# Hyena convolutions on one core: second-stage products of 512 columns, block turns spread over four chunks, and a capped stream of filter pieces

## The chip, the cores and the metric

The kernel runs on one core of one Trainium2 chip. The metric is the device time of one execution in microseconds; the time of a kernel is the median of its runs. The engines are named as in the profile: PE (TensorE, matmuls and transposes through the array), DVE (VectorE), ACT (ScalarE), POOL (GpSimd) and SP (SyncE, which here only issues DMAs).

## What is computed

One layer of a hybrid encoder on a sequence of 2048 positions: a Hyena branch and an RWKV branch side by side, joined by gates, then a feed-forward block. The change touches only the Hyena branch, after the projection of its input `u` to 3 x 512 channels:

```python
def long_conv(z, h_fwd, h_bwd, d_skip):
    L = z.shape[1]
    n = 2 * L
    zf = jnp.fft.rfft(z, n=n, axis=1)
    hf = jnp.fft.rfft(h_fwd, n=n, axis=0) + jnp.conj(jnp.fft.rfft(h_bwd, n=n, axis=0))
    y = jnp.fft.irfft(zf * hf[None], n=n, axis=1)[:, :L]
    return y + z * d_skip

def hyena_mixer(u, conv_w, conv_b, ..., skip):
    u = short_conv3(u, conv_w, conv_b)
    v, x1, x2 = jnp.split(u, 3, axis=-1)
    h = hyena_filters(L, ...)
    z = x1 * long_conv(v, h[:, 0, 0], h[:, 0, 1], sk[0])
    return x2 * long_conv(z, h[:, 1, 0], h[:, 1, 1], sk[1])
```

Each of the two long convolutions is made for four blocks of 128 channels: eight products of spectra in all. `hyena_filters` makes the filters from positions: sines, a matrix product and a decaying window.

## The kernel before

The stage is the function `hyena`, some 500 of 3946 us. A Fourier transform of 4096 points is made as matmuls in two stages of 128 x 32. The loop runs over eight products k = 0 to 7 and in each over eight chunks q = 0 to 7 of 128 x 512 numbers; (k,q) is chunk q of product k. In a chunk PE does, in this order:

- T (`times`): second stage of the transform of the signal, `second(V)`, into a PSUM tile `pz`. DVE multiplies it by the filter's spectrum H (the tile A, L1339) and by H with blocks of 32 partitions exchanged (the tile B, L1340). The exchange (Hs) is four DMAs from SP, L1329.
- L (`load`): the same for the spectrum of the filter, two chunks ahead, `second(Vf)`; ACT copies it to H.
- Q (`added`): the product back through the inverse of the second stage, for the chunk before, into `pq`; ACT copies it to Q.
- then the work that `beside` has put into the chunk, a list of functions per chunk.

`second` makes four matmuls of 128 columns (one weight, `Mc[:, 3]`, but `Mc[:, 0]` for the very first 128 columns of the spectrum), `added` eight. The matmuls are f32, and the trace has two records of each. The work beside:

- F: one of the 16 pieces of a filter: g0 g1 f0 g2 f1 ... g7 f6 f7. A g is a PE product (L1240, `pg`) that DVE multiplies by the window (L1244); an f is its first transform stage (L1226, `pf`), which needs the result of that g; ACT copies it (L1228) and sends it to DRAM as Hd (L1229, a DMA from ACT's queue). `given` (L1319) reads Hd back as Vf once all 16 pieces are made.
- turns: `turned`, four per product: four transposes on PE into `ph` (tag po, two PSUM buffers) and an ACT copy (L1286). They turn a row of 128 channels for the next product.
- U: `onward`, the first transform stage of the next product (L1294, matmuls on 64 rows, `pfz`); ACT copies.
- V: block transpositions of 32 x 32 on DVE (L1303, 2.1 to 2.3 us each). Four belong to the way back (`piece`, chunks 0 and 1) and four to the next product (`flipped`); T of (k+1,0) needs all four of the latter.
- i, v and gate: the last inverse stage (L1358), and in the products of the second convolution (k = 3, 4, 7) the turn back on PE (L1365, `pv`, buffers shared with `pq`) and the multiplication by x2 on DVE (L1370).
- conv: a block of 512 positions of the short convolution: ACT (L1183), then DVE (L1184, L1189).

The PSUM tag pf has two buffers, shared by pg, pf and pfz. On PE, ACT, DVE and SP the order of this stage is the order of the program text (`manual_schedule`): an instruction that waits holds all behind it on its engine. In product 6, `ready` adds the splitting of the weights of the next stage (`weights_on`: ACT and DVE, wl<-wr), in product 7 `late_inputs` the rest of it.

Of the kernel before, what the change touches and what calls it, by code (L numbers as in the profile page):

```python
# [190 lines left out]
class Layer:  # L191
# [943 lines left out]
    def next(self, name):  # L1135
        first, n = dict(w=(8, 3), A=(12, 2), B=(0, 2), H=(2, 3), Hs=(5, 3))[name]
        k = self.turns[name]
        self.turns[name] = k + 1
        return self.ring(first + k % n).rearrange("p (a b) -> p a b", b=P)
# [125 lines left out]
    def hyena(self):  # L1265
# [3 lines left out]
        N = 2 * HT  # L1269
        E = mybir.EngineType  # L1270
        with tc.tile_pool(name="hy", bufs=1, reuse_waits="tile") as s, tc.tile_pool(name="hyp", bufs=2, space=PSUM, reuse_waits="tile") as ps, \
# [26 lines left out]
            def flips(U, k):  # L1298
# [4 lines left out]
                    nc.vector.transpose(V[:, :, sl].rearrange("p j c -> p c j"), U[:, :, sl].rearrange("p n c -> p c n"))  # L1303
                return V, piece

            def second(v, q):
                p = ps.tile([P, 4, P], F32, name="pz", tag="pz")
                for j in range(4):
                    mm(p[:, j], Mc[:, 0 if 4 * q + j == 0 else 3], v[:, j], start=True, stop=True)  # L1309
                return p  # L1310


# [30 lines left out]
            def added(i, q, Q):  # L1343
                A, B = AB.pop((i, q))
                p = ps.tile([P, 4, P], F32, name="pq", tag="pq")
                for j in range(4):
                    m = 0 if 4 * q + j == 0 else 3
                    mm(p[:, j], Mc[:, m + 1], A[:, j], start=True, stop=False)
                    mm(p[:, j], Mc[:, m + 2], B[:, j], start=False, stop=True)
                nc.scalar.copy(Q[:, 4 * q:4 * q + 4], p)  # L1350


# [38 lines left out]

            most = 15, 20, 24, 29, 36, 41, 46, 48

            def F():
                self.upto(self.pieces + 1)


            def beside(k, Q):
                at = {q: [] for q in range(8)}

                def put(q, *fs):
                    at[q] += fs

                def conv():
                    if self.blocks < most[k]:
                        next(self.conv)

                on = k + 1 < N
                c, o = PRODUCTS[k - 1] if k else (1 - 2, 1)
                new = {}  # L1410

                def turned(q, src):
                    if q == 0:
                        new["z"] = zt(src)
                        new["o"] = self.z1 if k == 0 else self.short(HT + c if o == 0 else c + 2)
                    turn(new["o"], new["z"], q)

                def onward(q):
                    if q == 0:
                        new["U"] = self.pre(k + 1)  # L1420
                    fwd(new["z"], new["U"], q)

                def flipped(q):
                    if q == 0:
                        Vs[k + 1], new["f"] = flips(new["U"], k + 1)
                    new["f"](q)

                if k:
                    VQ, piece = flips(Q, k + 1)
                    f = [lambda q=q: piece(q) for q in range(4)]  # L1430
                    put(0, f[0], F, F, f[1], F)
                    put(1, f[2], F, F, f[3], F)
                else:
                    put(0, F, F, conv, F)
                    put(1, F, F, conv, F)
                t = [lambda q=q: turned(q, "x1" if k and o == 0 else "z") for q in range(4)]
                u = [lambda q=q: onward(q) for q in range(4)]
                if k and o == 0:
                    def inner(q):
                        if q == 0:  # L1440
                            new["x"], new["z"] = new["z"], zt("z")
                        p = inverse(VQ, q)
                        tt(out=new["z"][:, 4 * q:4 * q + 4], in0=p, in1=new["x"][:, 4 * q:4 * q + 4], op=ALU.mult)

                    n = [lambda q=q: inner(q) for q in range(4)]
                    put(1, t[0], t[1])
                    put(2, t[2], t[3], conv, n[0], n[1])
                    put(3, n[2], u[0], n[3], conv, u[1])
                    put(4, u[2], conv, u[3], F)
                else:  # L1450
                    if on:
                        put(1, t[0], t[1])
                        put(2, t[2], t[3])
                    if k:
                        result, turn_back, gated, ws = outward(k - 1, VQ)
                        r, b, g = ([lambda q=q, h=h: h(q) for q in range(4)] for h in (result, turn_back, gated))
                        if k > 3:
                            put(1, conv)
                        put(2, r[0], conv, r[1], F)
                        if on:  # L1460
                            put(3, r[2], u[0], r[3], b[0], conv, g[0], u[1])
                            put(4, b[1], u[2], g[1], b[2], u[3], conv, g[2], F)
                            put(5, b[3])
                        else:
                            put(3, r[2], b[0], r[3], g[0], b[1])
                            put(4, g[1], b[2], g[2], b[3], g[3])
                    else:
                        put(2, conv)
                        put(3, u[0], u[1], conv)
                        put(4, u[2], conv, u[3], F)  # L1470
                if on:
                    f = [lambda q=q: flipped(q) for q in range(4)]
                    put(5, f[0], F, F, conv, F)
                    if k and o:
                        put(5, g[3])
                    put(6, f[1], F, F, f[2], F)
                    if k == 4:
                        put(6, conv)
                    put(7, f[3], F, conv, F)
                return at  # L1480

# [10 lines left out]
            for q in range(4):  # L1492
                piece(q)
                if q < 2:
                    load(0, q)
                F()
                F()
            for k in range(N):
                Qs[k] = self.pre(k)
                at = beside(k, Qs.get(k - 1))  # L1500
                if k == N - 2:
                    self.ready(at)
                if k == N - 1:
                    self.late_inputs(at, ps)
                for q in range(8):
                    times(k, q, Vs[k])
                    n, r = divmod(q + 2, 8)
                    if k + n < N:
                        load(k + n, r)
                    if k or q:  # L1510
                        added(*((k, q - 1, Qs[k]) if q else (k - 1, 7, Qs[k - 1])))
                    for f in at[q]:
                        f()
                    if q in (3, 6) and k + 1 < N:
                        given(k + 1, q // 4)
            added(N - 1, 7, Qs[N - 1])
            self.outputs()
            VQ, piece = flips(Qs[N - 1], N)
# [16 lines left out]
    def ready(self, at):  # L1535
        nc = self.nc

        def first():
            self.wr = [self.xp1.tile([P, 8, 4, P], F32R, name=f"w{n}", tag=f"x{n}", bufs=1) for n in "hl"]
            self.wraws = [self.weights_raw("r", dt) for dt in range(2)]  # L1540

        at[4].append(first)
        for dt, q in enumerate((5, 6, 6, 7, 7)):
            at[q].append(lambda dt=dt: self.weights_on(dt))

    def weights_on(self, dt):
# [5 lines left out]
    def late_inputs(self, at, ps):  # L1552
        nc = self.nc

        def loads():
            row = self.pre(0)
            self.gates = row[:, 0:14]
            self.yraw = row[:, 16:24].rearrange("p a b -> p (a b)").rearrange("p (k t) -> p k t", t=TB)
            nc.sync.dma_start(self.yraw, self.yrd[:, :, 0:TB].rearrange("c p t -> p c t"))
            for dt in range(7):  # L1560
                nc.sync.dma_start(self.gates[:, 2 * dt:2 * dt + 2].rearrange("p a b -> p (a b)"), self.gated[8 + dt, :, 0:TB])

        def parts():
            hl = [self.wp.tile([P, 4, TB], F32R, name="y", tag="wh", bufs=2) for k in range(2)]
            self.split(*hl, self.yraw)
            self.yr = [(hl[0][:, k], hl[1][:, k]) for k in range(4)]

        def gates():
            nc.scalar.activation(self.gates, self.gates, AF.Tanh, scale=0.5)
            self.rs = [self.wp.tile([P, 4, TB], F32, name="rs", tag="wraw", bufs=2)]  # L1570

        for q in range(3):
            at[q].append(lambda q=q: self.weights_on(5 + q))
        at[2].append(loads)
        at[4].append(parts)
        at[4].append(gates)
        for q in range(3):
            at[5 + q].append(lambda q=q: self.right(ps, q))
# [298 lines left out]
```

## Time and profile before

| | us |
|---|---|
| three runs | 3939.88, 3943.91, 3944.74 (median 3943.91) |
| profiled execution | 3947.99 |
| its span | 3946.2 |
| PE busy in the span | 3801.3 (96%) |
| DVE busy, ACT busy | 2346.6 (59%), 1456.8 (37%) |
| starts of T(k,0), k = 0 to 7 | 1627.60, 1680.74, 1740.35, 1799.89, 1862.47, 1926.95, 1988.40, 2044.46 |

The profile shows one execution. A busy PE is not PE at its best: matmuls are pipelined, so the distance from start to start tells what one costs, and the granted clock of a stretch (1.00 is 2.4 GHz, 0.50 is 1.2 GHz) stands beside it. In the timeline "x8" is eight records, that is four f32 matmuls; a transpose through PE has one record.

### The profile page before, as it was taken

How to read it: one execution, taken by the hardware profiler on the slowest of the kernel's cores; microseconds unless marked ns; L12 is line 12 of the kernel's file. 1: busy time of each engine (PE TensorE's matmuls, PEld its weight loads, DVE VectorE, ACT ScalarE, POOL GpSimd, SP SyncE). 2: the span in 40 equal slices, each digit the busy share in tenths (PEclk: the TensorE clock that was granted, in tenths of full speed). 3: DMA queues.
4: the chain of work that ended last, by engine and by line, in shares of the span. 5: the costliest groups of instructions: out<-in, count | busy, mean ns of one | idle time of the engine just before them, and what ended most of it. 6: DMA issues, size and time to landing. Idle time of an engine off the chain costs nothing.

```text
span 3946.2 us, 64945 instructions
## 1 busy us (share of the span) xinstructions
PE 3801.3 (96%) x26152; PEld 3128.1 (79%) x26152; DVE 2346.6 (59%) x3734; ACT 1456.8 (37%) x2851; POOL 93.1 (2%) x139
## 2 busy tenths in 40 slices
PE   8999999999999998899988999999999999999998
PEld 6766557787777787899887999788888878888887
DVE  5466884666667775577676555544444474444444
ACT  3345663333335566655543333211111151111113
POOL 0000001111010100000000000000000000000000
PEclk9999999999999999899999999999999999999999
DMA  4556878677777777545555443411111142111111
GB/s 140 173 167 172 222 212 247 193 225 206 216 221 223 215 209 216 128 124 141 138 148 180 130 126 110 155 48 49 49 50 51 49 139 69 49 48 48 49 48 43
DMA packets 426420, 535.43 MB, mean 136 GB/s; under 512 B 137268, under 2 KB 305725, under 8 KB 423365
## 3 DMA queue, kind: packets, MB, share of 16 engines
q1 hardware_dynamic: 365703, 459.91, 40.1%
q10 hardware_dynamic: 54528, 54.59, 4.5%
q0 software_dynamic: 5888, 16.78, 1.6%
q8 instruction: 206, 3.38, 0.4%
q14 instruction: 95, 0.78, 0.1%
HBM read 369.52 MB, written 144.70 MB: 130 GB/s over the span
## 4 chain that ended last, share of the span: by engine, by line
PE 51%; DVE 3%; DMA 2%; ACT 1%; issue 1%; SPq 0%; ACTq 0%; DVEq 0%
PE pg L205 4%; PE pg L203 4%; PE pu L203 4%; PE pu L204 4%; PE pg L204 4%; PE pu L205 4%; PE pd L203 4%; PE pd L205 4%; PE pd L204 4%; PE pz L1309 2%; PE pm L203 1%; PE pm L204 1%; PE pm L205 1%; PE po L204 1%; PE po L205 1%; PE po L203 1%
## 5 line engine op out<-in xcount | busy, mean ns | idle before, releaser
L203 PE MATMUL acc<-xh,wh 128*128 128x512 f32 x1376 | 577.3, 420 | 9.4 <-ACT xh L198 8.4
L204 PE MATMUL acc<-xl,wh 128*128 128x512 f32 x1376 | 547.0, 398 | 3.9 <-DVE xl L199 3.8
L205 PE MATMUL acc<-xh,wl 128*128 128x512 f32 x1376 | 547.0, 398 | 0.8 <-DVE wl L199 0.8
L1814 DVE TENSOR_TENSOR acc<-pd,acc 128x1024 f32<-128x1024 f32 x320 | 387.6, 1221 | 69.3 <-PE pd L205 63.6
L198 ACT CAST fwh<-raw 128x1024 fp32r<-128x1024 f32 x132 | 138.6, 1050 | 704.6 <-PE pg L204 487.5
L203 PEld LDWEIGHTS acc<-xh,wh 128*128 128x128 f32 x1376 | 261.6, 190 | 120.4 <-issue 47.9
L1842 DVE TENSOR_TENSOR h<-pu,sg 128x512 f32<-128x512 f32 x88 | 60.9, 692 | 476.6 <-PE pu L205 470.8
L204 PEld LDWEIGHTS acc<-xl,wh 128*128 128x128 f32 x1376 | 262.3, 191 | 63.5 <-DVE xl L199 6.5
L205 PEld LDWEIGHTS acc<-xh,wl 128*128 128x128 f32 x1376 | 261.9, 190 | 62.6 <-DVE wl L199 2.1
L203 PE MATMUL pd<-fwh,hh 128*128 128x512 f32 x704 | 275.6, 391 | 2.8 <-DVE acc L1812 2.4
L205 PE MATMUL pd<-fwh,hl 128*128 128x512 f32 x704 | 274.9, 390 | 0.0
L204 PE MATMUL pd<-fwl,hh 128*128 128x512 f32 x704 | 274.8, 390 | 0.0
L203 PE MATMUL pu<-fxh,fwh 128*128 128x512 f32 x704 | 274.3, 390 | 0.5 <-ACT fxh L1728 0.5
L203 PE MATMUL pg<-fxh,fwh 128*128 128x512 f32 x704 | 274.1, 389 | 0.2 <-DVE fxl L1729 0.2
L205 PE MATMUL pg<-fxh,fwl 128*128 128x512 f32 x704 | 274.2, 389 | 0.0
L205 PE MATMUL pu<-fxh,fwl 128*128 128x512 f32 x704 | 274.1, 389 | 0.0
L204 PE MATMUL pu<-fxl,fwh 128*128 128x512 f32 x704 | 274.0, 389 | 0.0
L204 PE MATMUL pg<-fxl,fwh 128*128 128x512 f32 x704 | 273.9, 389 | 0.0
L199 DVE TENSOR_TENSOR fwl<-raw,fwh 128x1024 fp32r<-128x1024 f32 x132 | 161.1, 1221 | 166.6 <-ACT fwh L198 162.7
L199 DVE TENSOR_TENSOR wl<-wraw,wh 128x512 fp32r<-128x512 f32 (+1 forms) x217 | 169.3, 791 | 138.7 <-ACT wh L198 132.1
L198 ACT CAST wh<-wraw 128x512 fp32r<-128x512 f32 (+1 forms) x217 | 150.2, 704 | 221.2 <-PE acc L204 176.7
L203 PEld LDWEIGHTS pd<-fwh,hh 128*128 128x128 f32 x704 | 132.0, 188 | 41.0 <-DVE acc L1814 12.2
(290 smaller groups left out, 7490.4 us busy)
## 6 DMA issues: line engine op xcount, KB each, us to landing
wraw<-in_w_in SPq DMA_DIRECT2D x130, 512.0 KB
ABp<-ABd SPq DMA_DIRECT2D x64, 512.0 KB
raw<-in_fg SPq DMA_DIRECT2D x44, 512.0 KB
raw<-in_fu SPq DMA_DIRECT2D x44, 512.0 KB
raw<-in_fd SPq DMA_DIRECT2D x44, 512.0 KB
ud<-ev ACTq DMA_DIRECT2D x84, 256.0 KB
ABd<-AB SPq DMA_DIRECT2D x32, 512.0 KB
gated<-ev SPq DMA_DIRECT2D x64, 256.0 KB
```

The source lines that it names most:

```text
L198: nc.scalar.copy(hi, src)
L199: nc.vector.tensor_tensor(out=lo, in0=src, in1=hi.bitcast(F32), op=ALU.subtract)
L203: mm(ps, ah, bh, start=start, stop=False)
L204: mm(ps, ah, bl, start=False, stop=False)
L205: mm(ps, al, bh, start=False, stop=stop)
L1309: mm(p[:, j], Mc[:, 0 if 4 * q + j == 0 else 3], v[:, j], start=True, stop=True)
L1814: tt(out=acc[t], in0=pf, in1=acc[t], op=ALU.add)
L1842: tt(out=h, in0=put, in1=sg, op=ALU.mult)
```

## The change

1. `second` and `added` make one or two matmuls of 512 columns instead of four or eight of 128, for every chunk with q > 0. For q = 0 they are as before.
2. The lists of `beside`: all four turns of a product stand in chunk 1 (two were in chunk 2); `onward` in chunks 2 and 3 (3 and 4); `flipped` one to a chunk in chunks 4 to 7 (chunk 5 one, chunk 6 two, chunk 7 one); turns back and gates of the second convolution somewhat later.
3. F makes a piece only up to a number per product, `made`. The pieces stand two, three, three and two in chunks 4 to 7 and then three in each of chunks 0 and 1; none in chunks 2 and 3. `given(k + 1, 0)` moves from the end of chunk 3 to the start of chunk 4's list.
4. `ready` starts in chunk 5 (4) and splits four groups of weights in product 6 (five); `late_inputs` four in product 7 (three).

```diff
             def second(v, q):
                 p = ps.tile([P, 4, P], F32, name="pz", tag="pz")
-                for j in range(4):
-                    mm(p[:, j], Mc[:, 0 if 4 * q + j == 0 else 3], v[:, j], start=True, stop=True)
+                if q:
+                    mm(flat(p), Mc[:, 3], flat(v), start=True, stop=True)
+                else:
+                    for j in range(4):
+                        mm(p[:, j], Mc[:, 3 if j else 0], v[:, j], start=True, stop=True)
...
             def added(i, q, Q):
...
+                if q:
+                    mm(flat(p), Mc[:, 4], flat(A), start=True, stop=False)
+                    mm(flat(p), Mc[:, 5], flat(B), start=False, stop=True)
...
-            def F():
-                self.upto(self.pieces + 1)
+            made = 43, 58, 74, 90, 106, 122, 128, 128
...
+                def F():
+                    self.upto(min(self.pieces + 1, made[k]))
...
                     n = [lambda q=q: inner(q) for q in range(4)]
-                    put(1, t[0], t[1])
-                    put(2, t[2], t[3], conv, n[0], n[1])
-                    put(3, n[2], u[0], n[3], conv, u[1])
-                    put(4, u[2], conv, u[3], F)
+                    put(1, *t)
+                    put(2, n[0], n[1], conv, u[0])
+                    put(3, n[2], u[1], n[3], conv, u[2], u[3])
...
+                    if on:
+                        put(1, *t)
+                        put(1, *[conv] * (k > 3))
+                        put(2, r[0], u[0], r[1], conv, u[1])
+                        put(3, r[2], u[2], r[3], b[0], conv, u[3], g[0])
+                        put(4, b[1], b[2], g[1])
+                        put(5, b[3], g[2])
+                        put(6, g[3])
...
                     f = [lambda q=q: flipped(q) for q in range(4)]
-                    put(5, f[0], F, F, conv, F)
-                    if k and o:
-                        put(5, g[3])
-                    put(6, f[1], F, F, f[2], F)
-                    if k == 4:
-                        put(6, conv)
+                    put(4, f[0], F, conv, F)
+                    put(5, f[1], F, F, conv, F)
+                    put(6, f[2], F, F, *[conv] * (k == 4), F)
                     put(7, f[3], F, conv, F)
...
+                    if q == 4 and k + 1 < N:
+                        given(k + 1, 0)
                     for f in at[q]:
                         f()
-                    if q in (3, 6) and k + 1 < N:
-                        given(k + 1, q // 4)
+                    if q == 6 and k + 1 < N:
+                        given(k + 1, 1)
...
-        at[4].append(first)
-        for dt, q in enumerate((5, 6, 6, 7, 7)):
+        at[5].append(first)
+        for dt, q in enumerate((6, 6, 7, 7)):
...
-        for q in range(3):
-            at[q].append(lambda q=q: self.weights_on(5 + q))
+        for q in range(4):
+            at[q].append(lambda q=q: self.weights_on(4 + q))
```

In the lists of matmuls below, "x4" counts instructions, and ph, pg, pf, pz, pq, po, pfz are the PSUM tiles named above. PE at the end of (2,1) and the start of (2,2), in the program before:

```order
5427 L1349 MATMUL pq<-rg,Mc 128x128
5428 L1226 MATMUL pf<-rg,Fc 128x128 x4
5429 L1240 MATMUL pg<-fw_17261,H3b 128x128 x4
5430 L1226 MATMUL pf<-rg,Fc 128x128 x4
5431 L1285 MATMUL ph<-k_c_ident,co 128x128 x8
5432 L1309 MATMUL pz<-V,Mc 128x128 x4
5433 L1309 MATMUL pz<-Vf,Mc 128x128 x4
5434 L1348 MATMUL pq<-rg,Mc 128x128
5435 L1349 MATMUL pq<-rg,Mc 128x128
```

and in the changed one:

```order
5342 L1359 MATMUL pq<-rg,Mc 128x128
5343 L1240 MATMUL pg<-fw_17249,H3b 128x128 x4
5344 L1226 MATMUL pf<-rg,Fc 128x128 x8
5345 L1285 MATMUL ph<-k_c_ident,co 128x128 x16
5346 L1312 MATMUL pz<-V,Mc 128x512
5347 L1312 MATMUL pz<-Vf,Mc 128x512
5348 L1353 MATMUL pq<-rg,Mc 128x512
5349 L1354 MATMUL pq<-rg,Mc 128x512
5350 L1368 MATMUL po<-V,Gc 64x128 x16
```

Two turns (x8) became four (x16), and the three pieces f g f became g f f; the second f of the pair needs DVE's result of the g in front of them.

PE at the end of (2,6) and the start of (2,7) before:

```order
5494 L1348 MATMUL pq<-rg,Mc 128x128
5495 L1349 MATMUL pq<-rg,Mc 128x128
5496 L1226 MATMUL pf<-rg,Fc 128x128 x4
5497 L1240 MATMUL pg<-fw_18015,H3b 128x128 x4
5498 L1226 MATMUL pf<-rg,Fc 128x128 x4
5499 L1309 MATMUL pz<-V,Mc 128x128 x4
5500 L1309 MATMUL pz<-Vf,Mc 128x128 x4
5501 L1348 MATMUL pq<-rg,Mc 128x128
```

and in the changed program, the whole of (2,6):

```order
5374 L1312 MATMUL pz<-V,Mc 128x512
5375 L1315 MATMUL pz<-Vf,Mc 128x128 x4
5376 L1353 MATMUL pq<-rg,Mc 128x512
5377 L1354 MATMUL pq<-rg,Mc 128x512
5378 L1240 MATMUL pg<-fw_17689,H3b 128x128 x4
5379 L1226 MATMUL pf<-rg,Fc 128x128 x4
5380 L1240 MATMUL pg<-fw_17689,H3b 128x128 x4
5381 L1312 MATMUL pz<-V,Mc 128x512
5382 L1312 MATMUL pz<-Vf,Mc 128x512
```

The pieces f g f became g f g.

DVE in product 6, from A of (6,4) to the second half of (6,6)'s start, before:

```order
2222 L1339 TENSOR_TENSOR rg<-pz,rg 128x512
2223 L1340 TENSOR_TENSOR rg<-pz,rg 128x512
2224 L1184 SCALAR_TENSOR_TENSOR co<-cu_16369,k_conv,co 128x512
2225 L1189 SCALAR_TENSOR_TENSOR co<-cu_16369,k_conv,co 128x512
2226 L1339 TENSOR_TENSOR rg<-pz,rg 128x512
2227 L1340 TENSOR_TENSOR rg<-pz,rg 128x512
2228 L1303 STREAM_TRANSPOSE V<-U 128x32x32
2229 L1184 SCALAR_TENSOR_TENSOR co<-cu_16347,k_conv,co 128x512
2230 L1189 SCALAR_TENSOR_TENSOR co<-cu_16347,k_conv,co 128x512
2231 L199 TENSOR_TENSOR wl<-wr,wh 128x512
2232 L1339 TENSOR_TENSOR rg<-pz,rg 128x512
2233 L1340 TENSOR_TENSOR rg<-pz,rg 128x512
```

and in the changed program:

```order
2218 L1345 TENSOR_TENSOR rg<-pz,rg 128x512
2219 L1346 TENSOR_TENSOR rg<-pz,rg 128x512
2220 L1303 STREAM_TRANSPOSE V<-U 128x32x32
2221 L1184 SCALAR_TENSOR_TENSOR co<-cu_16369,k_conv,co 128x512
2222 L1189 SCALAR_TENSOR_TENSOR co<-cu_16369,k_conv,co 128x512
2223 L1345 TENSOR_TENSOR rg<-pz,rg 128x512
2224 L1346 TENSOR_TENSOR rg<-pz,rg 128x512
2225 L1303 STREAM_TRANSPOSE V<-U 128x32x32
2226 L1184 SCALAR_TENSOR_TENSOR co<-cu_16347,k_conv,co 128x512
2227 L1189 SCALAR_TENSOR_TENSOR co<-cu_16347,k_conv,co 128x512
2228 L1345 TENSOR_TENSOR rg<-pz,rg 128x512
2229 L1346 TENSOR_TENSOR rg<-pz,rg 128x512
```

V of the next product's first block stands one chunk earlier, behind A and B of (6,4), and no chunk has two; the split of weights wl<-wr is gone from (6,5).

## Rows read from the trace of the kernel before

**Rows 1.** The table of stretches (busy us and number of records of each engine; the last three columns are the granted clock of PE, the DMA share and GB/s), a stretch that holds most of product 2 and one at the end of product 6 and in product 7.

```profile
1740.00:1800.00 60.00, 57.53 (x531) 55.13 (x532) 42.66 (x50) 33.38 (x73) 0.00 (x0) 1.00 0.51 128
2040.00:2090.00 50.00, 41.55 (x368) 39.95 (x369) 36.88 (x45) 18.11 (x29) 0.00 (x0) 0.93 0.51 145
```

**Rows 2.** The waits of PE in the stage, 1600 to 2115 us (line that waited, who released it: us in total, times, longest).

```profile
PE pz L1309 <- DVE V L1303: 13.6, 7, 5.9
...
PE pg L1240 <- ACT cu L1228: 4.1, 6, 0.7
PE pg L1240 <- DVE rg L1244: 2.9, 3, 1.1
...
PE pf L1226 <- DVE rg L1244: 1.5, 1, 1.5
...
PE po L1358 <- ACT x L1286: 1.2, 4, 0.3
...
PE po L1358 <- ACT z L1286: 0.6, 2, 0.3
```

**Rows 3.** The timeline (start, busy us, engine, line, out<-in, records; in brackets the idle time before it and who ended it) of PE in products 2, 3 and 4, and after it of DVE in products 2 and 3.

```profile
1780.80 1.06 PE L1309 MATMUL pz<-V,Mc 128*128 128x128 f32 x8
...
1848.66 1.16 PE L1240 MATMUL pg<-fw,H3b 128*128 128x128 f32 x8 [1.14 <-DVE rg L1244]
...
1911.21 1.16 PE L1240 MATMUL pg<-fw,H3b 128*128 128x128 f32 x8 [1.10 <-DVE rg L1244]
...
1788.24 0.75 DVE L1184 SCALAR_TENSOR_TENSOR co<-cu,k_conv,co 128x512 f32<-128x512 f32 x1 [2.01 <-ACT co L1183]
1789.03 0.75 DVE L1189 SCALAR_TENSOR_TENSOR co<-cu,k_conv,co 128x512 f32<-128x512 f32 x1
...
1845.82 2.24 DVE L1303 STREAM_TRANSPOSE V<-U 128x1024 f32<-128x1024 f32 x1
```

**Rows 4.** The timeline of PE in chunk 7 of product 2 and at the start of product 3.

```profile
1793.58 1.06 PE L1309 MATMUL pz<-V,Mc 128*128 128x128 f32 x8
1794.47 1.06 PE L1309 MATMUL pz<-Vf,Mc 128*128 128x128 f32 x8
...
1798.04 1.06 PE L1226 MATMUL pf<-rg,Fc 128*128 128x128 f32 x8
1799.89 1.13 PE L1309 MATMUL pz<-V,Mc 128*128 128x128 f32 x8 [0.79 <-DVE V L1303]
```

**Rows 5.** An f32 line of 512 columns elsewhere in the kernel, L535: its own view (duration in ns, least, median and most), and one of its places in the timeline of PE.

```profile
L535 PE MATMUL pp<-ksum,k_c_bones x32: 592/594/595, 267.6 to 621.0; 128*128 128x512 f32 x32
...
267.61 1.02 PE L535 MATMUL pp<-ksum,k_c_bones 128*128 128x512 f32 x2
```

**Rows 6.** The timeline at the start of product 2: PE where (2,0) starts, then DVE in (2,0) and (2,1).

```profile
1740.35 1.13 PE L1309 MATMUL pz<-V,Mc 128*128 128x128 f32 x8 [1.13 <-DVE V L1303]
...
1744.81 2.23 DVE L1303 STREAM_TRANSPOSE V<-U 128x1024 f32<-128x1024 f32 x1 [1.14 <-ACT U L1350]
...
1747.51 2.25 DVE L1303 STREAM_TRANSPOSE V<-U 128x1024 f32<-128x1024 f32 x1
1749.64 0.67 DVE L1244 TENSOR_TENSOR rg<-pg,rg 128x512 f32<-128x512 f32 x1
1750.20 0.70 DVE L1339 TENSOR_TENSOR rg<-pz,rg 128x512 f32<-128x512 f32 x1
1751.58 0.69 DVE L1340 TENSOR_TENSOR rg<-pz,rg 128x512 f32<-128x512 f32 x1 [0.68 <-DMA rg<-rg]
1752.19 2.28 DVE L1303 STREAM_TRANSPOSE V<-U 128x1024 f32<-128x1024 f32 x1
1754.36 0.65 DVE L1244 TENSOR_TENSOR rg<-pg,rg 128x512 f32<-128x512 f32 x1
```

**Rows 7.** The timeline of ACT in (2,1): the copy of a filter piece and the copies of turned blocks behind it (x2).

```profile
1754.50 0.56 ACT L1228 COPY cu<-pf 128x512 f32<-128x512 f32 x1
...
1755.50 1.07 ACT L1286 COPY x<-ph 128x512 f32<-128x512 f32 x2 [0.44 <-ACT cu L1228]
```

**Rows 8.** The timeline at the end of the stage: DVE at the end of (6,4) and in (6,5), DVE ahead of (7,0), and PE at (7,0).

```profile
2026.66 0.75 DVE L1184 SCALAR_TENSOR_TENSOR co<-cu,k_conv,co 128x512 f32<-128x512 f32 x1 [4.36 <-ACT co L1183]
...
2029.45 2.26 DVE L1303 STREAM_TRANSPOSE V<-U 128x1024 f32<-128x1024 f32 x1
...
2042.13 2.18 DVE L1303 STREAM_TRANSPOSE V<-U 128x1024 f32<-128x1024 f32 x1
...
2044.46 2.05 PE L1309 MATMUL pz<-V,Mc 128*128 128x128 f32 x8 [5.86 <-DVE V L1303]
```

**Rows 9.** The table of stretches (columns as in the first group): (2,1), then one behind the matmuls on 64 rows in (5,4), and two around the start of product 7; last, the timeline of PE in (5,4).

```profile
1747.62:1754.79 7.17, 7.17 (x66) 7.17 (x65) 6.49 (x6) 3.92 (x11) 0.00 (x0) 1.00 0.48 136
1966.00:1970.00 4.00, 4.00 (x20) 3.76 (x20) 1.92 (x4) 1.47 (x5) 0.00 (x0) 0.60 0.97 218
1970.00:1974.00 4.00, 4.00 (x37) 4.00 (x36) 3.58 (x4) 1.79 (x5) 0.00 (x0) 0.97 0.17 45
2040.00:2044.40 4.40, 0.00 (x0) 0.00 (x0) 4.40 (x6) 1.97 (x4) 0.00 (x0) 0.72 0.62 194
2044.40:2048.00 3.60, 3.54 (x16) 3.57 (x17) 3.50 (x7) 0.15 (x1) 0.00 (x0) 0.50 1.01 218
...
1962.69 2.99 PE L1294 MATMUL pfz<-z,Fz 64*128 64x128 f32 x27
```

More of the change, by code (lines that the diff above doesn't have):

```diff
@@ L1304, in flips @@
                 return V, piece
+            flat = lambda v: v.rearrange("p a b -> p (a b)")
             def second(v, q):
                 p = ps.tile([P, 4, P], F32, name="pz", tag="pz")
-                for j in range(4):
-                    mm(p[:, j], Mc[:, 0 if 4 * q + j == 0 else 3], v[:, j], start=True, stop=True)
+                if q:
[3 more added lines that the diff above has]
+                        mm(p[:, j], Mc[:, 3 if j else 0], v[:, j], start=True, stop=True)
                 return p
@@ L1345, in added @@
                 p = ps.tile([P, 4, P], F32, name="pq", tag="pq")
[L1346 to L1349, printed above, removed]
+                if q:
+                    mm(flat(p), Mc[:, 4], flat(A), start=True, stop=False)
+                    mm(flat(p), Mc[:, 5], flat(B), start=False, stop=True)
+                else:
+                    for j in range(4):
+                        m = 3 if j else 0
+                        mm(p[:, j], Mc[:, m + 1], A[:, j], start=True, stop=False)
+                        mm(p[:, j], Mc[:, m + 2], B[:, j], start=False, stop=True)
                 nc.scalar.copy(Q[:, 4 * q:4 * q + 4], p)
@@ L1445, in beside @@
                     n = [lambda q=q: inner(q) for q in range(4)]
-                    put(1, t[0], t[1])
-                    put(2, t[2], t[3], conv, n[0], n[1])
-                    put(3, n[2], u[0], n[3], conv, u[1])
-                    put(4, u[2], conv, u[3], F)
-                else:
[L1451 to L1470, printed above, removed]
@@ new lines, in beside @@
+                    put(1, *t)
+                    put(2, n[0], n[1], conv, u[0])
+                    put(3, n[2], u[1], n[3], conv, u[2], u[3])
+                elif k:
+                    result, turn_back, gated, ws = outward(k - 1, VQ)
+                    r, b, g = ([lambda q=q, h=h: h(q) for q in range(4)] for h in (result, turn_back, gated))
+                    if on:
[6 more added lines that the diff above has]
+                        put(6, g[3])
+                    else:
+                        put(1, conv)
+                        put(2, r[0], conv, r[1])
+                        put(3, r[2], b[0], r[3], g[0], b[1])
+                        put(4, g[1], b[2], g[2], b[3], g[3])
+                else:
+                    put(1, *t)
+                    put(2, u[0], conv, u[1])
+                    put(3, u[2], conv, u[3])
@@ L1495, in hyena @@
                     load(0, q)
-                F()
-                F()
+                self.upto(self.pieces + 2)
             for k in range(N):
```

## The prediction, made before the result

> **What bounds the kernel now.** Outside the convolution stage both programs stand in the same order, so I read the stage alone. The table of stretches comes first: TensorE (PE) computes for about 57 of 60 us in a usual product and 41.6 of 50 us at the end [rows 1]. Inside the stage PE therefore sets the time, except at the end. Next the waits of PE [rows 2]: nothing large, only many small waits that come back in every product, apart from 5.9 us in which PE waits for DVE's last transposition ahead of product 7. I write (k,q) for chunk q of product k. Counted out of the group's times, the list is: six waits for the last transposition at (k,0), k = 1 to 6, 13.6 - 5.9 = 7.7 us; six for ACT's copy of a filter piece, 4.1; six for the copies of turned blocks at (k,2), 1.2 + 0.6 = 1.8; one of 1.5 at (1,1); and 2.2 at (3,5) and (4,5) [rows 3]. That is 17.3 us in 21 waits. A wait is a little longer than its row says, since the row begins at the modelled end of the last matmul: the piece that starts at 1798.04 would let the next start 0.89 later, at 1798.93, and the next starts at 1799.89, so 0.96 are lost where the row shows 0.79 [rows 4]. With 0.17 added to each of the 21, the present order loses 17.3 + 3.6 = 20.9 us.
>
> **The wide products.** Four f32 matmuls of 128 columns hold PE for 0.89 us, start to start [rows 4]. A 512-column f32 matmul is two records; two of them last 1.02 and one 0.59, so they start 0.43 apart, and the product costs 0.86 [rows 5]. Per chunk with q > 0 a product saves 0.03. The change makes 224 such groups (112 of `second`, 112 in `added`). Some 40 lie in the last four chunks of product 6 and in product 7, where PE waits for DVE; the other 184 give **-5.5 us**. No engine but PE is touched by this edit. For bounds: 512 columns could go no faster than 0.86 by any f32 row here, so -6.7 with all 224 on the path; were the saving lost in longer waits for DVE, 0.
>
> **The waits that leave.** Filter pieces change places, f g f for g f g at (k,0), and no wait for ACT is left there; the four block turns are one to a chunk, in chunks 4 to 7, so that DVE has one transposition instead of two in chunk 6 and is done before (k+1,0) starts; all turns come in chunk 1, so their copies are done by chunk 2. All 21 waits go: **-20.9 us**. The bound is half of it for the first group: were DVE late again by what stands below, 4 to 8 us of it would stay.
>
> **The waits that come.** (a) (k,1), k = 2 to 6: the last two pieces f6, f7 now stand in the chunk whose g7 they need. f7 needs DVE's product of g7. Along DVE's queue from the start of (2,0) at 1740.35: the first V starts 4.46 later, by the copy of Q that it needs (say 4.3 with narrower Q); then V 2.13, product 0.57, V 2.13, A 0.57, B 0.60, V 2.17 and the product of g7 0.57 [rows 6]: 13.1. PE has reached f7 at 6.14 for (2,0) and T, L, Q, g, f of 0.86 + 0.86 + 1.78 + 0.89 + 0.89, that is 11.4. So PE waits 1.7 to 1.8, five times: **+8.8**. The B in these rows waited another 0.68 for its DMA; each such wait would be on the path now, and I keep it for the range. (b) Then come four turns in a row, with two PSUM buffers between them. The third needs ACT's copy of the first; that copy stands behind the copy of f7 and the DMA issue after it, and starts 1.0 after that copy [rows 7]. PE needs 0.43 for a turn, so it waits 1.05, five times: **+5.3**. (c) (0,1) and (1,1) are f f g and the turns; the second f waits as the one at (1,1) does now, 1.5 to 1.7 [rows 2]: 2 x 1.75 = **+3.5**. (d) (k,6) is now g f g. Its second g takes the PSUM buffer that DVE's product of the first g must empty. That product stands behind the convolution of chunk 5, which starts 1788.24 - 1780.80 = 7.4 into that chunk and takes 1.5 [rows 3], behind A, B and a V: 2.8 + 0.6 + 0.6 + 2.15 + 0.6 = 6.75 into chunk 6, plus 0.2 to pass it on, where PE is ready after 5.2. That is 1.75 for k = 2 and 5, and 3.0 for k = 3 and 4, whose queue has a gate of 1.05 as well: **+9.5**. The same mechanism is seen now at (3,5), 1.1 for one product behind a V [rows 3]. (e) (k,5), k = 3, 4: the fourth turn back takes the buffer that gate 2 empties, behind some 2 us of chunk 4's DVE work: **+4.0**. (f) Smaller ones of kind (d) at (0,5) and (1,5): **+2.1**. Together **+33.2 us**. None of these waits exists in the profile, so the size is an estimate; if DVE and ACT catch up in each wait, as they do at (k,0) now, half is left (+16.6), and with the DMA waits of B it is +37.
>
> **The end of the stage.** The transposition of product 6's first block starts at 2029.45, in (6,5); before that DVE waits 4.36 us for work [rows 8]. From there A, B, convolutions, V and weight splits run almost without a break to 2044.3, and PE waits from 2038.6 on. With `onward` two chunks earlier, that transposition (2.15 us) and the chain behind it start inside the empty 4.36, and one split moves behind product 7's third chunk. From (6,2) to (7,0) I find 36.8 us where now there are 41.6: **-4.8**; in product 7 the moved split leaves **-0.5**. The bounds are 0 (the convolutions in chunk 5, which wait for ACT, hold the chain where it is) and -5.9, the whole wait.
>
> **The clock.** From 1966 to 1970 the granted clock is 0.60, with PE busy all four microseconds; PE did 20 records where the stretch behind it has 37, about 2 us lost [rows 9]. No wait stands ahead of it, but the 64-row products do, and they move to chunks 2 and 3. I count **-2.0** for it; left where it is, 0.
>
> **Sum.** -5.5 - 20.9 + 33.2 - 4.8 - 0.5 - 2.0 = -0.5 us. The profiled execution took 3947.99 us; it lies 4.1 above the median of the runs, and no term hangs on that. From the median: 3943.9 - 0.5 = **3943 us**. The change gives back in new waits for DVE and ACT what it takes out.
>
> **Rivals.** Faster: the new waits are half as long. In each of them DVE goes on working and comes into the next chunk with less in its queue, so (d), (e) and (f) are worth a few tenths each. For it: in the present order such a queue is worked off within a chunk, and DVE computes only 42.7 of 60 us [rows 1]. Against it: the chain of (a) is counted along one queue and has no slack. Worth -15.6, with a bit more or less: about 3928; it decides when the second g of (k,6) waits under 1 us. Slower: the clock. (k,1) becomes a wait, a piece, two turns, a wait, two turns, and PE is left for 2.8 us of 10.7 with nothing. The rows show the clock fallen to 0.72 in a stretch where PE waited 4.4 us, and 0.50 in the one behind it, where 16 records took the time of twice as many: 2 us lost [rows 9]. They also show it at 1.00 in (2,1), with two turns and no wait. If it falls behind the four turns of five to six products, it costs 2 each: 3943 + 11 = 3954. It decides if the half level (1.2 GHz) is seen in (k,1) to (k,2).
>
> The Trainium skill ("TensorE: Matmul & The Clock Gate", Part 4: PE-mode transpose) says that a transpose does not count as PE-busy for the clock in the way a matmul does. By that rule the turns lengthen each pause in (k,1), and this rival is the likelier one; no stretch of this trace has four turns in a row.
>
> Slower in another way: SP, which issues the shifted copies for B, is held by the scattered writes of filter pieces. B waits 0.68 at (2,1) now [rows 6]; with two f in each of (k,0) and (k,1) it may be 1 to 2 later in five products: about 3950. Not what it says: the 512-column products cost as much as four of 128; then 3943 + 5.5, about 3949.
>
> **Chances.** Under 0.2% (7.9 us) a measurement of this kernel can hardly be told from no change. The forecast within it: 0.50. Shorter waits, 3928: 0.24. Clock, 3954: 0.14. B's copies, 3950: 0.08, half of it over the line. No cheaper wide products, 3949: 0.04, inside it. So faster 0.24, same 0.58, slower 0.18. The range leaves out the lower third of the first rival and the dearer half of the second: 3929 to 3955.
>
> **What would show it.** (a) A PE wait for DVE's product of g7 of about 1.6 in each (k,1), k > 1, and one of 0.9 for ACT's copy of a turn. (b) At (k,0) no wait for V or for ACT. (c) In (k,6) a wait of a second g for DVE, longer at k = 3, 4. (d) 512-column f32 records 0.43 apart. (e) (7,0) about 36.8 behind (6,2). (f) The clock at 1.00 through (k,1). The forecast is wrong if (a) and (c) are under half of this, if the clock falls, or if the wide products start other than 0.86 apart.

## The result

| | runs | median, us (lowest to highest) | ratio to before (95%) |
|---|---|---|---|
| before | 22 | 3942.34 (3929.98 to 3951.87) | |
| changed | 22 | 3953.89 (3943.22 to 3959.21) | 1.0028 (1.0019 to 1.0037) |

The change makes the kernel 11 us slower (7.5 to 14.6). In the profiled executions T(7,7) starts 466.9 us behind T(0,0), where it was 457.0: the stage alone accounts for 9.9.

The waits of PE in the changed kernel, 1620 to 2062 us, answer to [rows 2] (same columns):

```profile
PE pg L1240 <- DVE rg L1244: 13.1, 8, 3.0
PE pf L1226 <- DVE rg L1244: 9.3, 5, 2.5
PE pz L1315 <- DMA Vf<-Hd: 4.4, 1, 4.4
PE ph L1285 <- ACT z L1286: 3.7, 3, 1.5
PE pv L1375 <- DVE co L1380: 3.6, 2, 1.8
PE ph L1285 <- ACT x L1286: 3.2, 4, 0.8
PE pz L1315 <- ACT wh L198: 2.5, 1, 2.5
PE pg L1240 <- ACT rg L1228: 1.4, 2, 0.7
...
PE pz L1315 <- DVE V L1303: 0.2, 1, 0.2
```

The waits for V (but for 0.2 at (2,0)) and for the copies of turned blocks at (k,2) are gone, as is the wait for ACT's copy at (k,0), except that (1,0) has a new one (0.7 of the 1.4; the other 0.7 was there at (0,0)). The new waits (a), (b), (d), (e) and (f) stand there. (c) came in another form: PE waits in (0,1) and (1,1) for ACT's copy of a turn, 1.3 and 0.7 us, not for DVE. Two kinds were in no term of the sum: 4.4 us for Vf at (6,6), and 0.2 twice for ACT's copy of U in (3,4) and (4,4). Of the eight waits in the first row, two of 0.7 stand ahead of T(0,0). Ahead of (7,0) 2.5 of 5.9 are left.

The wide products, in the timeline of PE in (2,7), answer to [rows 4, 5]:

```profile
1797.04 1.02 PE L1312 MATMUL pz<-V,Mc 128*128 128x512 f32 x2
1797.90 1.02 PE L1312 MATMUL pz<-Vf,Mc 128*128 128x512 f32 x2
1798.76 1.02 PE L1353 MATMUL pq<-rg,Mc 128*128 128x512 f32 x2
1799.62 1.02 PE L1354 MATMUL pq<-rg,Mc 128*128 128x512 f32 x2
1800.47 1.05 PE L1226 MATMUL pf<-rg,Fc 128*128 128x128 f32 x8
```

They start 0.86 apart, as forecast. (2,1) in the timeline of PE, and its transposed blocks' copies in that of ACT, answer to [rows 6, 7]:

```profile
1752.67 1.06 PE L1226 MATMUL pf<-rg,Fc 128*128 128x128 f32 x8
1755.34 1.13 PE L1226 MATMUL pf<-rg,Fc 128*128 128x128 f32 x8 [1.61 <-DVE rg L1244]
1756.30 1.04 PE L1285 MATMUL ph<-k_c_ident,co 128*128 128x128 f32 x8
1758.17 1.15 PE L1285 MATMUL ph<-k_c_ident,co 128*128 128x128 f32 x8 [0.83 <-ACT x L1286]
1759.15 1.02 PE L1312 MATMUL pz<-V,Mc 128*128 128x512 f32 x2
...
1756.50 0.59 ACT L1228 COPY rg<-pf 128x512 f32<-128x512 f32 x1 [2.15 <-PE pf L1226]
...
1757.53 1.08 ACT L1286 COPY x<-ph 128x512 f32<-128x512 f32 x2 [0.44 <-PE ph L1285]
```

f6 lets f7 start at 1753.56; it starts at 1755.34, 1.78 later. Then two turns, a wait until the first of them is copied, and the other two. The end of the stage, PE, SP and ACT in product 6, answers to [rows 8]:

```profile
2041.53 1.02 PE L1312 MATMUL pz<-V,Mc 128*128 128x512 f32 x2
2046.97 2.05 PE L1315 MATMUL pz<-Vf,Mc 128*128 128x128 f32 x8 [4.42 <-DMA Vf<-Hd]
...
2057.24 2.04 PE L1315 MATMUL pz<-V,Mc 128*128 128x128 f32 x8 [2.51 <-ACT wh L198]
...
2037.19 2.41 SPq L1335 DMA_DIRECT2D rg<-rg  x4
2039.69 1.92 SPq L1325 DMA_DIRECT2D Vf<-Hd  x4
...
2046.30 0.91 SPq L1629 DMA_DIRECT2D wr<-in_w_rw  x2
...
2049.10 0.59 ACT L1331 COPY rg<-pz 128x512 f32<-128x512 f32 x1 [6.08 <-issue]
...
2051.81 1.14 ACT L198 CAST wh<-wr 128x512 fp32r<-128x512 f32 x2
```

Vf is asked for at 2039.69, 5.1 us into (6,4) and behind that chunk's Hs copies; PE wants it 2.7 us later and gets it 7.3 us later. (The wait at 2057.24 is put down to ACT's cast, which had long ended; T needs the last V.) Last the table of stretches: (2,1) and (3,1), each with four turns, then the second half of (3,6) with the start of (3,7), and the same place in product 4; they answer to [rows 9]:

```profile
1748.27:1759.15 10.88, 8.44 (x62) 7.01 (x61) 9.10 (x8) 6.04 (x15) 0.00 (x0) 1.00 0.50 141
1808.45:1819.95 11.50, 8.45 (x62) 7.02 (x61) 9.04 (x8) 6.04 (x15) 0.00 (x0) 1.00 0.52 143
...
1861.50:1867.00 5.50, 4.63 (x13) 3.11 (x14) 2.48 (x5) 0.58 (x3) 0.00 (x0) 0.69 0.79 231
...
1929.00:1934.00 5.00, 3.73 (x11) 2.66 (x12) 3.81 (x7) 1.36 (x5) 0.00 (x0) 0.66 0.94 248
```

PE idles 2.4 to 3.3 us in each (k,1), k = 2 to 6, and the clock stays at 1.00 there in this execution. It falls behind the single waits of 2.8 and 3.0 us at (3,6) and (4,6).

### The profile page after: what moved, and what is told of

Its sections match the earlier page's. It is cut to its first block, busy times and chain, and to the rows that moved or that the text cites. A ratio compares the mean times of both kernels' runs of the same rounds, so it can differ in the third digit from the quotient of the medians.

```text
span 3955.8 us, 62273 instructions
## 1 busy us (share of the span) xinstructions
PE 3800.3 (96%) x24808; PEld 3012.4 (76%) x24808; DVE 2348.0 (59%) x3734; ACT 1457.8 (37%) x2851; POOL 93.3 (2%) x139
## 4 chain that ended last, share of the span: by engine, by line
PE 50%; DVE 3%; DMA 2%; ACT 2%; issue 1%; SPq 0%; ACTq 0%; DVEq 0%
PE pg L203 4%; PE pg L205 4%; PE pg L204 4%; PE pu L203 4%; PE pu L204 4%; PE pu L205 4%; PE pd L203 4%; PE pd L205 4%; PE pd L204 4%; PE pz L1312 2%; PE pm L203 1%; PE pm L204 1%; PE pm L205 1%; PE po L205 1%; PE po L204 1%; PE po L203 1%
```

## The experiments

Lines and rows are named as before; "(7,0) behind (6,2)" is the distance of the starts of their T in the profiled execution. Each kernel ran 9 to 12 times, the last two five times. Times are told as ratios to the kernel before, with the interval; the changed kernel is 1.0028.

**The two parts apart.** The kernel before with the first part of the diff only, and the changed kernel without it (`if False` for `if q` in `second` and `added`).

> The kernel before with the products of 512 columns alone. Theory: 0.03 us less in each of the 184 groups where PE sets the pace, no new waits, 5.5 us less than before. Rival 1 (PE reaches its waits for DVE and ACT earlier and waits longer there): 2 us less at most, with longer rows for V at (k,0). Rival 2 (wide products bring the falls of the clock): the granted clock is under 1.00 in a stretch of products 1 to 5 in which it was 1.00 before, and the time is that of before or more.

Measured: 0.9979 (0.9968 to 0.9991), median 3935.94. Chunks in which PE never waits are 0.10 to 0.14 shorter (0.07 in chunk 1, whose Q is still narrow), as four groups of 0.03 make them, and no wait in products 0 to 5 is longer by more than 0.3. The first rival falls by the time, though the six waits at (k,0), k = 1 to 6, are 1 us longer in all. The clock was at half for 6 us behind the wait of 3.0 us at (5,0), where before a wait of 2.9 was followed by none; that is the second rival's sign, without its result.

> The changed kernel with the products of 128 columns of before in all chunks: the new lists alone. Theory (the lists bring the loss): 5.5 us more than the changed kernel, about 17 more than before, the waits at (k,1), (k,5) and (k,6) each shorter by 0.1 at most, and the clock falls behind the waits of 3 us at (3,6) and (4,6) as it does in the changed kernel. Rival (the wide products bring the falls of the clock): the clock is 1.00 in (3,6) to (4,7) and the time is within 3 us of the changed kernel's.

Measured: 1.0037 (1.0024 to 1.0051), 3956.62. The lists lose, some 15 us against before, 19 where the wide products are in both kernels (1.0028 against 0.9979). The clock stayed up at (3,6) and (4,6), behind waits of 2.7 and 2.9 us. The same two stretches as above, counted from the ends of these waits:

```profile
1855.87:1861.37 5.50, 4.62 (x41) 4.63 (x42) 4.05 (x6) 1.14 (x3) 0.00 (x0) 1.00 0.98 307
1923.88:1928.88 5.00, 3.73 (x33) 3.73 (x34) 4.96 (x9) 2.01 (x6) 0.00 (x0) 1.00 0.98 338
```

That is the sign of the rival, and its time (a median 2.7 us above the changed kernel's) is at the edge of its bound. So the lists bring the loss without any fall of the clock ahead of (6,6), and behind these waits the clock fell only where the wide products are. Apart, the two parts come to some 6 us, together to 11; the difference has the size of the falls, but the intervals do not settle it.

**The late read of Vf.**

```diff
-                    if q == 4 and k + 1 < N:
-                        given(k + 1, 0)
                     for f in at[q]:
                         f()
-                    if q == 6 and k + 1 < N:
-                        given(k + 1, 1)
+                    if q in (3, 6) and k + 1 < N:
+                        given(k + 1, q // 4)
```

> The changed kernel with the first half of the next filter's spectrum read at the end of chunk 3 again instead of in chunk 4. Theory (the read is issued too late in product 6, where chunks 4 and 5 hold no pieces and last 7 us): PE's wait of 4.4 us for Vf at (6,6) is gone, ACT's and DVE's weight split no longer stands behind it, (7,0) starts 37 to 37.5 us behind (6,2) instead of 40.6, and the kernel takes 3 us less than the changed one. Rival (DVE's chain of transpositions and splits sets (7,0) in any case): the wait goes, (7,0) still starts 40 us or more behind (6,2), and the time stays.

Measured: 1.003 (1.002 to 1.0041), 3953.01; no gain. The wait at (6,6) is gone, but (7,0) still starts 40.2 behind (6,2). The timeline of ACT, SP and PE says why:

```profile
2053.09 0.62 ACT L198 CAST wh<-wr 128x512 fp32r<-128x512 f32 x1 [4.98 <-DMA wr<-in_w_rw]
...
2048.56 0.91 SPq L1627 DMA_DIRECT2D wr<-in_w_rw  x2
...
2059.04 2.05 PE L1315 MATMUL pz<-V,Mc 128*128 128x128 f32 x8 [6.84 <-DVE V L1303]
```

ACT now waits 5 us for the weights, which `ready` asks for one chunk later than before; DVE's split stands behind it, and the last V behind the split. In the other products the order on PE, DVE and ACT is that of the changed kernel, but the build gave the second g of (k,6) the other of the two PSUM buffers, that of the f ahead of it: it waits 0.84 for ACT's copy, and (3,6) and (4,6) last 7.1 instead of 10.0. So the wait there is one for that buffer. The time did not fall for it. In this execution DVE stood 5.0 us in (4,0), because ACT's step of the convolution waited 4.6 for a DMA (0.5 in the changed kernel), and 4.3 in (5,1), where B waited for its copies. The clock fell behind both, and in (2,1) and (3,1) behind waits of 2.1 us for g7. In order, ACT in (4,0), DVE in (5,1) and the stretch behind the wait in (2,1):

```profile
1870.73 0.81 ACT L1183 ACTIVATE co<-cu,k_conv 128x512 f32<-128x512 f32 x1 [4.58 <-DMA yhd<-co]
...
1950.24 0.69 DVE L1346 TENSOR_TENSOR rg<-pz,rg 128x512 f32<-128x512 f32 x1 [4.28 <-DMA rg<-rg]
...
1754.20:1758.20 4.00, 4.00 (x20) 3.60 (x20) 1.98 (x1) 1.64 (x3) 0.00 (x0) 0.57 0.35 96
```

The rival's numbers came, but not by its reason: the next run shows that DVE's chain does not need that time.

**Both reads of product 6 early.** `given(7, 0)` at the end of (6,3), and in `ready`:

```diff
-        at[5].append(first)
+        at[4].append(first)
```

> The changed kernel with two reads of product 6 issued as early as before: the first half of product 7's spectrum at the end of chunk 3, and the first two blocks of the next stage's weights in chunk 4 instead of 5. Only product 6 changes. Theory (the end of the stage was lengthened by these two reads, one after the other: with the first alone put back, ACT waited 5 us for the weights instead): no wait for Vf at (6,6), no wait of ACT for the weights over 1 us, (7,0) 36.5 to 38 us behind (6,2) instead of 40.6, and 3 to 4 us less for the kernel. Rival (DVE's transpositions and convolutions alone need that time): (7,0) 40 us or more behind (6,2).

Measured: 1.0021 (1.0011 to 1.0031), (7,0) 37.2 behind (6,2). The times of this kernel and of the changed one overlap; the 3.4 us at (7,0) are read from the traces. With Vf alone put back the weights were late; with both, neither is, and the last V waits for DVE's own queue (the row puts PE's wait down to ACT's cast, which ends at the same time; DVE's last V ends at 2053.51). In the timeline of SP and PE, Vf goes out at 2033.60 and the weights at 2041.38:

```profile
2033.60 3.07 SPq L1325 DMA_DIRECT2D Vf<-Hd  x4
...
2041.38 0.91 SPq L1631 DMA_DIRECT2D wr<-in_w_rw  x2
...
2042.18 1.16 PE L1315 MATMUL pz<-Vf,Mc 128*128 128x128 f32 x8
...
2053.65 2.05 PE L1315 MATMUL pz<-V,Mc 128*128 128x128 f32 x8 [3.86 <-ACT wh L198]
```

**The convolution out of DVE's way.**

```diff
-                    put(3, n[2], u[1], n[3], conv, u[2], u[3])
+                    put(3, n[2], u[1], n[3], conv, u[2], u[3], conv)
...
-                    put(5, f[1], F, F, conv, F)
+                    put(5, f[1], F, F, F)
```

and the same at the ends of the other two lists of chunk 3.

> The changed kernel with the convolution block of chunk 5 put at the end of chunk 3's list, where DVE has little to do. Theory (the second piece g of chunk 6 waits because DVE's product of the first stands behind that convolution): the waits of 1.6 and 1.9 at (2,6) and (5,6) are under 0.4, those of 2.9 and 3.2 at (3,6) and (4,6) fall to 1.0 to 1.7, the clock stays at 1.00 there, and the kernel takes 7 to 10 us less than the changed one. Rival (DVE's queue only moves): the second g still waits over 1 us, or T of the next product waits for its transposition by as much, and the time stays within 3 us.

Measured: 1.004 (1.0025 to 1.0055); no gain, and the rival holds in that DVE's queue only moved, though not to the places it named. (2,6), (3,6) and (4,6) are 0.8 to 2.9 shorter and 0.9 to 1.3 longer than (k,6) without a wait (6.2), but (0,5) and (1,5) are 1.0 and 1.2 longer, (3,5) 2.6, (5,1) 2.2, (4,1) 1.3 and (6,6) 1.9, partly with the clock at half. In product 3 DVE stands idle for 6 us in chunk 3, but the moved block is the last of that chunk and runs only in (3,4), at 1845.84. From there DVE has no break until gate 2 in (3,5), which comes 1 us later than in the changed kernel, counted from T of (3,4); half the clock behind PE's wait makes up most of the rest. The waits of PE, 1742 to 1950 us, and the moved block on DVE:

```profile
PE pf L1226 <- DVE rg L1244: 5.8, 3, 2.6
PE pv L1375 <- DVE co L1380: 2.8, 1, 2.8
PE pg L1240 <- DVE rg L1244: 1.8, 2, 1.1
...
1845.84 0.74 DVE L1184 SCALAR_TENSOR_TENSOR cv<-cu,k_conv,cv 128x512 f32<-128x512 f32 x1
```

**The turns around f7.**

```diff
-                    put(1, f[2], F, F, f[3], F)
+                    put(1, f[2], F, F, f[3])
...
-                    put(1, *t)
+                    put(1, t[0], t[1], F, t[2], t[3])
```

(the second in both lists that have a V ahead of it.)

> The changed kernel with the last piece f7 between the second and the third turn of chunk 1, instead of ahead of all four. Theory (PE waits 1.7 to 2.6 us for DVE's product of g7, then 1 us for ACT's copy of the first turn): two turns fill 0.9 us of the first wait and their copies are done by the end of it; the wait for DVE is 0.8 to 1.7, the wait for ACT is gone, each (k,1) with k = 2 to 6 is 1.9 us shorter, and the kernel takes 7 to 10 us less than the changed one, if that time isn't given back. Rival (DVE's queue sets what follows): (k,1) is shorter, but PE waits as much more behind it, for the transposition that the first inverse block of (k,2) needs or in (k,5) and (k,6), and the time stays within 3 us.

Measured: 1.0005 (0.9995 to 1.0016), 9 us less than the changed kernel. In (2,1) the two turns fill the wait, and what is left of it ends with a copy, not with DVE (in (4,1) and (5,1) 1.8 and 1.4 us for DVE are left):

```profile
1748.03 1.06 PE L1226 MATMUL pf<-rg,Fc 128*128 128x128 f32 x8
1748.92 1.04 PE L1285 MATMUL ph<-k_c_ident,co 128*128 128x128 f32 x8
1750.77 1.13 PE L1226 MATMUL pf<-rg,Fc 128*128 128x128 f32 x8 [0.81 <-ACT x L1286]
1751.73 1.04 PE L1285 MATMUL ph<-k_c_ident,co 128*128 128x128 f32 x8
1752.61 1.02 PE L1312 MATMUL pz<-V,Mc 128*128 128x512 f32 x2
```

(2,1) lasts 8.98 instead of 10.88, the five together 10 us less, and (k,2) is as it was.

**The stream of pieces back.** One piece less in chunk 4, f7 in chunk 2:

```diff
-            made = 43, 58, 74, 90, 106, 122, 128, 128
+            made = 43, 57, 73, 89, 105, 121, 128, 128
...
-                    put(2, n[0], n[1], conv, u[0])
+                    put(2, n[0], n[1], conv, u[0], *[F] * (k > 1))
...
-                        put(2, r[0], u[0], r[1], conv, u[1])
+                        put(2, r[0], u[0], r[1], conv, u[1], F)
...
-                    put(4, f[0], F, conv, F)
+                    put(4, f[0], *[F] * (k == 0), conv, F)
```

> The changed kernel with the stream of filter pieces one piece later, which is nearly that of before: one piece in chunk 4, f7 in chunk 2, pieces f g f in chunk 6 and g f g in chunk 0. All turns, first stages, transpositions and gates stay where the change put them. Theory (f7 behind its own g7, and the second g of chunk 6 behind DVE's product, are what the lists lose): the waits for DVE in (k,1) and (k,6) are gone (18 us), with them the falls of the clock at (3,6) and (4,6) (3 us); waits for ACT at (k,0) of 0.84 come back (4 us), and the kernel takes 12 to 17 us less than the changed one, 0 to 6 less than before. Rival (the turns, the earlier first stages and the gates lose as much as the stream): 6 us less than the changed one or fewer, still slower than before.

Measured: 1.0 (0.999 to 1.001), 11 us less than the changed kernel, level with before. (k,6) is 6.2 for k = 2 to 5 (product 6 still waits for Vf), (k,1) 9.1 to 9.5: f7's wait is gone, but the wait of the third turn is still there, and the pieces g f g now stand in (k,5) and (1,6), which are 0.8 to 2.0 longer.

> As the run before the last, and the four turns two in chunk 1 and two in chunk 2, as in the kernel before; the first stages, the transpositions one to a chunk and the gates stay where the change put them. Theory (four turns in a row cost 1 us in each product, for ACT's copy of the first): 3 us less than with the stream alone put back, since 1.0 in each (k,1) is gone and 0.45 in each (k,2) is back. Rival (a third turn in the same chunk costs nothing once f7 is out of it): the same time within 2 us.

Its edit on top: `put(1, t[0], t[1])` and `t[2], t[3]` at the head of chunk 2's list, for products 1 to 6. Measured: 0.9979 (0.997 to 0.9988), 8 us less again, more than expected. (k,1) is 7.1, and (k,1) with (k,2) 1.1 shorter, not 0.55; in the trace the stage is 5.9 shorter.

**Everything that lost, undone.** The two last edits and the two early reads in one kernel; then the turns of product 0 split as well.

> Stream and turns back as in the run before the last, and the two early reads of product 6: what is left of the change is the wide products, the first stages of the next product a chunk earlier, the transpositions one to a chunk and the later gates. Theory (the losses of the stream, of the turns and of the two late reads add up, each in its place): (7,0) 38 to 40 us behind (6,2) where it is 43.1 with the reads late, 3 to 4 us less than with stream and turns alone, that is 10 to 13 us less than the kernel before. Rival (with the reads early, DVE's chain makes PE wait for the last transposition ahead of (7,0) by as much): within 1.5 us of the run with stream and turns back.

Measured: 0.9964 (0.9951 to 0.9976), median 3926.82: 14 us less than before (9 to 19), with the next run the fastest of the study. (7,0) is 39.6 behind (6,2), where it was 43.1 with the reads late. Its waits of PE, 1610 to 2050 us:

```profile
PE pg L1240 <- DVE rg L1244: 8.7, 8, 1.7
PE pz L1315 <- ACT wh L198: 3.9, 1, 3.9
PE pz L1312 <- DVE rg L1346: 3.7, 3, 2.5
PE pg L1240 <- ACT cu L1228: 3.4, 5, 0.7
...
PE pz L1315 <- DVE V L1303: 1.4, 1, 1.4
```

> As the run before, and the four turns of product 0 two in chunk 1 and two in chunk 2 as well. Theory (a third turn waits for ACT's copy of the first): the 1.5 us in (0,1) are gone, T(1,0) is 1.0 to 1.5 us nearer to T(0,0), and the kernel is that much faster, which the times can't tell. Rival (in product 0 the wait only moves to the first stage in (0,2), which needs the turned blocks): T(1,0) stays where it is, within 0.3 us.

Measured: 0.9966 (0.9952 to 0.9979); T(1,0) is 1.6 nearer to T(0,0), (0,1) 2.5 shorter and (0,2) 0.9 longer.

## Why the prediction was wrong

The forecast was -0.5 us; +11 was measured. The mechanism stood in the main: the stage gave up its old waits and got new ones for DVE and ACT. Two steps failed, and the new waits were put too small. That the clock rival's figure, 3954, is the one measured is luck: by the trace the clock brought some 3 of the 11 us ahead of the end of the stage, and in another chunk than the rival named.

| term of the sum | forecast | measured |
|---|---|---|
| wide products | -5.5 | 0.86 for 0.89 in each group; alone -0.21%, -8 (-13 to -3.5) |
| waits that leave | -20.9 | all but 0.3 at (2,0); 0.84 is new at (1,0): -19.7 |
| (a) f7 behind g7, five | 8.8 | 9.3 + 5 x 0.17 = 10.1 |
| (b), (c) turns | 5.3 + 3.5 | 6.9 + 7 x 0.17 = 8.1 |
| (d), (f) second g, six | 9.5 + 2.1 | 11.8 + 6 x 0.17 = 12.8 |
| (e) fourth turn back | 4.0 | 3.6 + 2 x 0.17 = 3.9 |
| copy of U at (3,4), (4,4) | none | 0.5 + 2 x 0.17 = 0.8 |
| (7,0) behind (6,2) | -4.8 | 40.6 for 41.6: -1.0 |
| product 7 | -0.5 | -1.2 |
| clock | -2.0 | +1.0 |

The right column, with -5.5 for the wide products, sums to 9.3, against 9.9 in the trace.

**The end of the stage** is the first step that failed, 3.8 us. The chain of V was read rightly: 37.2 with both reads early, where 36.8 was worked out. But the change issues two groups of DMAs later on SP's queue, the reads of `given(k + 1, 0)` behind one more chunk's Hs copies and the weights by a chunk, and neither stood in the sum. In products 0 to 5 there are twelve us or more from the start of chunk 4 to that of chunk 6; in product 6, without pieces, there are seven, and the read, issued 5 us into them, takes seven more. Half the clock followed the wait for it as well (2046.5 to 2050).

**The clock** is the second, 3 us. I counted the fall in (5,4) as gone, and it was, but new ones came behind the waits of 2.8 and 3.0 us of (d), which I had sized and not followed further: (3,6) with (3,7) and (4,6) with (4,7) are 1.4 and 1.5 us longer than in the lists alone, where nearly the same waits were followed by none. The rival had the mechanism and put it in (k,1); there the clock stayed at 1.00 in the changed kernel's trace. It is not safe there: in the traces of two kernels with the same order in (k,1) it fell, in (2,1) and (3,1) of the late read of Vf put back and in (4,1) of the moved convolution, behind waits of 2.1 to 2.6 us for g7. The Trainium skill ("TensorE: Matmul & The Clock Gate", Part 4: PE-mode transpose) says that a transpose does not count as PE-busy for the clock in the way a matmul does; the changed kernel's trace shows no fall behind the four turns in (2,1), with waits of 1.6 and 0.8 us around them, and in the other two kernels half the clock was there before the turns or with the first of them.

What the clock costs in the median is borne out in part. The mean granted clock, on record for each run, is 0.9845 over the 22 runs of the changed kernel, and 0.9861, 0.9861 and 0.9864 over those of the kernel before (30), the lists alone (10) and the wide products alone (12). From 0.9861 to 0.9845 is 0.0016 of 3954 us: an estimate of some 6 us if all of it fell on a busy PE, and less where PE was idle. That the falls need the lists and the wide products together fits these means, but is not shown.

**The new waits** came out 2.5 us above the sum: (5,1) with 2.6 for f7, (f) with 3.2 for 2.1, and the 0.8 for U. The second g of (k,6) was right, 9.6 for 9.5 (the 3.0 for k = 3 and 4 is 2.8 by its own terms, which makes 9.1). The rival of shorter waits falls by this. That the wide products gain and the lists lose is shown by the two parts alone.

The loss of the lists is settled by undoing: 1.0028 with all, 1.0000 without the stream, 0.9979 without the four turns in a row, 0.9964 without the late reads. So, undone in this order, the stream costs some 11 us, the turns 8, the reads 3 to 6. What is left of the change, the wide products, the first stages and transpositions a chunk earlier and the later gates, gains 14; the wide products alone gain 8. What stays open is why, in the run with Vf put back, the DMA ahead of (4,0) and B's copies in (5,1) took so much longer than in the changed kernel, and so why the shorter (k,6) brought no gain there.

## What to carry to other kernels

A consumer moved next to its producer turns a hidden latency into a wait on in-order queues; put other work of that engine between them, as the two turns between f6 and f7, worth 9 us here. When a list of steps is moved, count the DMAs that its functions issue, and look at the shortest stretch in which they must land, not at the usual one. Of several late things only the last shows as a wait: undo them together before calling one harmless.

## What was not expected

The same order of instructions on PE, DVE and ACT gave (3,6) of 10.0 and of 7.1 us, because the build chose the other of two PSUM buffers for one tile. A wait of PE of 2.1 to 3.0 us was followed by half the clock for 3 to 6 us in some places ((3,6) and (4,6) of the changed kernel, (2,1) with Vf put back, (5,0) with wide products alone) and by the full clock in others ((5,0) before, (3,6) and (4,6) of the lists alone, (5,1) of the changed kernel). Counted over all traces ahead of (6,6), waits of 2.0 to 3.0 us were followed by half the clock in 13 of 17 places in kernels with the wide products, and in none of five in the two kernels without them. It is one execution of each kernel, and no run was made to tell why.
